# A two-layer decoder trunk: table stores by ScalarE, a later split of y, a shared start of two products, and a new order around the norms

## The chip, the cores and the metric

The kernel runs on one core of a Trainium2 chip. The core has five engines that work side by side, each in the order of its own queue: TensorE (PE in the profile; its weight loads are PEld), VectorE (DVE), ScalarE (ACT), GpSimd (POOL) and SyncE (SP), which only issues transfers here. Transfers (DMA) can be issued by SP, ACT and POOL. The metric is the device time of one execution in microseconds (us). TensorE's clock can be reduced by a throttle; the profile shows what was granted, as a share of full speed.

## The reference, cut to what matters

The input is x, 256 positions of 2048 float32 values. There are two layers; each ends in `x <- LayerNorm(alpha * x + mixer(x))`.

```python
# layer 0: one input projection, two groups of heads
z, xbc, dt, q, k, v, gate = split(x @ in0_w)
xs, b, c = split(silu(causal_conv4(xbc)))          # b, c: 512 columns each
y_a = rms_norm((ssd_scan(xs * dt, dt * a, b, c) + d * xs) * silu(z))
y_b = attention(rotary(q), rotary(k), v) * silu(gate)
x   = layer_norm(alpha * x + concat(y_a, y_b) @ out0_w)
# layer 1: diagonal complex state space
u, gate = split(x @ in1_w)
y   = gelu(s5_scan(u) + d * u)                     # 128 groups of 16 channels, 64 complex states
ga, gb = split(y @ glu_w)
x   = layer_norm(alpha * x + (ga * sigmoid(gb) * silu(gate)) @ out1_w)
```

## The kernel before, in words

**Weight units.** All weights are cut into 432 units of 256 rows by 512 columns (512 KB). Units 0 to 207 are the input projection of layer 0: 26 products of 8 units, in the order b, c, xs (four products), z (four) and then q, k, v, gate for four groups of heads. Units 208 to 271 are its output projection (4 products of 16), 272 to 335 the input projection of layer 1 (u, then the gate), 336 to 399 the GLU, 400 to 431 the last projection. `split_to(i)` prepares units up to i: SP loads `raw` (L222, four buffers), ScalarE copies it to `wh` (L225), the part that TensorE's rounded float32 type keeps, and VectorE subtracts to get the rest, `wl` (L227). Unit 0 is done in two halves (L217, L218), with x in two small pieces (`xpart`). x is split in the same way into a high part (tile A) and a rest (tile B). The pieces 1 to 7 of x (256 KB each) are loaded by `early` ahead of weight units 1 to 7.

**Products.** `product(kind, ...)` calls `split_to(unit + 3)` ahead of each unit, so preparation runs three units ahead of TensorE. For each tile three matmuls are made: high by high, high by rest, rest by high. Kind "w" (`wmm`, L288) has 24 matmuls of 256 columns for a unit, kind "x" (`xmm`, L271) has 12 of 512. A product's results lie in PSUM banks (`banks`), two alternating sets.

**Small work.** Everything else waits in two lists. `jobs` is emptied by `pump` between the units of the current product, `back` at a steady pace up to a goal. `run` pins the first instruction of a job behind the splits of the unit that is two ahead (`issue_after`). The order written down is not final: the framework's scheduler orders each engine's queue after a simulated timeline, within dependencies and pins.

**Layer-1 tables.** The state-space layer works in 16 blocks. During layer 0, `block_jobs(b)` builds each block's tables: `bars` (load of bc, then bb), `efs` (tables et and, in ob, F: L676 to L686), `pes` (transposes of et by TensorE, L694 and L698, ScalarE's copy into ob, L699, then VectorE's kt, L705) and, for odd b, `mts` (om). The tile ob has two buffers, et and om one. `phasor_job` computes the phasor tables on GpSimd (L624 to L640, tile c). The tables are stored to DRAM (wb) by transfers that GpSimd issues: ob at L706, om at L719, c at L640.

**Layer 1.** The steps of the state-space scan are in `back`, in order of a step number: for block b, `load` (wt) at 2b-2, `enc` at 2b (TensorE on the input um, L1128), `rec1` and `rec2` (VectorE's recurrence gt, L1140 to L1156), `dec` (L1169, L1173) and `act` at 2b+4. For every fourth block the finished outputs are loaded back by GpSimd at 2b+6 (`y_load`, L1198, tile ut) and split by ScalarE and VectorE at 2b+8 (`y_split`, L1206 and L1207).

**Norm 0.** The last product of layer 0 is `product_apart`: two halves t of positions, one after the other. When half t is done, `after0` adds the residual, takes statistics and scales x (`scaled`, L1010 and L1013, on tile D), `mid` transposes eight column blocks of t = 0 ahead of the last matmuls of t = 1 (`turned`, transposes at L358, ScalarE's copy at L1023 into tile C, VectorE's rest at L1027 into tile F). Then come `warm(WARM1)`, two transposes of t = 1, `warm(WARM2)`, and the first unit of layer 1, in which `rest0` stands between the matmuls of `wh` by high x and `wl` by high x and those of `wh` by low x. Further column blocks are scaled and transposed at units 1, 3 and 5 of that product (`later`). `warm(n)` makes n matmuls of zeros (64 x 64) whose result nobody reads (L367); `warm(WARM0)` also stands at the start.

**End.** `after1` does the last residual, statistics and the reciprocal, then `piece(3)`, which ScalarE and GpSimd compute (L1293 to L1295), and pieces 0 to 2, two passes each on VectorE (L1297, L1298); each is stored by SP or ACT (L1299).

Of the kernel before, what the change touches and what calls it, by code (L numbers as in the profile page):

```python
# [24 lines left out]
WARM0 = 70  # L25
WARM1 = 30
WARM2 = 4
# [66 lines left out]
def _layout(inp):  # L94
# [12 lines left out]
    cols = [b, c, xs, z]  # L107
    for h in range(4):
        cols += [m[:, 512 * h : 512 * h + 512] for m in (q, k, v, g)]
    a["wi0"] = np.concatenate([_chunk(m) for m in cols], 0)  # L110
# [49 lines left out]
def trunk(tc, io, out):  # L160
# [8 lines left out]
    with ExitStack() as top:  # L169
# [31 lines left out]
        early = {}  # L201
        splits = {}
        keep = [None, range(0)]

        def split_to(i):
            while nsplit[0] <= min(i, len(units) - 1):
                n = nsplit[0]
                if n in early:
                    early.pop(n)()
                raw = st.tile([P, UK, 512], F32, tag="raw", name=nm("raw"))  # L210
                if n == 0:
                    wh = st.tile([P, UK, 512], F32R, tag="wh", name=nm("wh"))
                    wl = st.tile([P, UK, 512], F32R, tag="wl", name=nm("wl"))
                    for k in range(UK):
                        xpart(k)
                        nc.sync.dma_start(raw[:, k, :], units[n][:, k * 512 : k * 512 + 512])
                        A.activation(wh[:, k, :], raw[:, k, :], AF.Copy)  # L217
# [4 lines left out]
                nc.sync.dma_start(raw.rearrange("p k n -> p (k n)"), units[n])  # L222
# [4 lines left out]
                splits[n] = (high, V.tensor_tensor(wl, raw, wh.bitcast(F32), op=OP.subtract))  # L227
# [45 lines left out]
        def wmm(ps, u, nu, hl, wpair, late=None):  # L273
            pv = [p.rearrange("p (f n) -> p f n", n=S) for p in ps]
            wh, wl = wpair
            steps = [(j, o) for j in range(UK) for o in range(4)]
            if u == nu - 1:
                steps = [(j, o) for o in range(4) for j in range(UK)]
            for terms in ((0, 2), (1,)) if late else ((0, 1, 2),):
                if late and terms == (1,):  # L280
                    late()
# [10 lines left out]
        def product(kind, hl, nu=CU, prelude=None, late=None):  # L292
            ps = banks()
            for u in range(nu):
# [4 lines left out]
                if kind == "w":  # L299
                    wmm(ps, u, nu, hl, wpair, late if u == 0 else None)  # L300
# [9 lines left out]
        def product_pair(hl, between, after):  # L310
            pss = [banks(), banks()]
            for lo, hi in ((0, CU - 2), (CU - 2, CU)):
# [11 lines left out]
                if lo == 0:  # L324
                    between()

# [35 lines left out]
        G.memset(idle.bitcast(F32), 0.0)  # L362

        def warm(n):
            px = aux()
            for i in range(n):
                T.matmul(px[:64, 0:64], idle, idle, start=i == 0, stop=i == n - 1)  # L367
# [13 lines left out]
        with ExitStack() as l0:  # L381
# [24 lines left out]
            for i in range(1, CU):  # L406
                early[i] = xpiece(i)
# [110 lines left out]
            ps = product("w", xhl)  # L518
            conv_jobs(ps, 0, bT)
            jobs.append(dt_mm)  # L520
            jobs.extend(dt_jobs())
            ps = product("w", xhl)
            conv_jobs(ps, 4, cT)
# [120 lines left out]
            def block_jobs(b):  # L644
# [25 lines left out]
                def efs():  # L670
# [3 lines left out]
                    ob = h["ob"] = pp.tile([P, 1024], F32, tag="ob", bufs=2, name=nm("ob"))  # L674
# [4 lines left out]
                    V.tensor_copy(et[:, :, :, 3], bb[:, 0])  # L679
                    cp = [bc[:, 3, 4 * i : 4 * i + 4, :].unsqueeze(3).to_broadcast([P, 4, 16, 4]) for i in range(2)]  # L680
# [7 lines left out]
                def pes():  # L688
# [17 lines left out]
                    nc.gpsimd.dma_start(wb[b][:, 0:1024], ob)  # L706

                def mts():
# [12 lines left out]
                return [bars, efs, pes, mts] if b % 2 else [bars, efs, pes]  # L721
# [270 lines left out]
        with ExitStack() as lt:  # L992
# [41 lines left out]
            def after0(ps, t):  # L1034
# [8 lines left out]
                jobs.append((lambda: scaled(1, 2, 2)) if t else (lambda: scaled(0, 4, 4)))  # L1043
# [20 lines left out]
            later = {1: [(1, 1)], 3: [(0, 2), (1, 2)], 5: [(0, 3), (1, 3)]}  # L1064
            first1 = product("w", x1hl, prelude=lambda u: [step(t, i) for t, i in later.get(u, [])], late=rest0)
# [3 lines left out]
        with ExitStack() as l1:  # L1069
# [139 lines left out]
            for b in range(16):  # L1209
# [55 lines left out]
        with ExitStack() as l2:  # L1265
# [16 lines left out]
            def after1(ps, t):  # L1282
                def first():
                    res1(ps, 3, t)
                    norm_stats(st1, mr1, t)()
                    V.scalar_tensor_tensor(mr1[:, t, 3:4], mr1[:, t, 0:1], -1.0, mr1[:, t, 2:3], op0=OP.mult, op1=OP.mult)

                def piece(i):
                    def go():
                        sl = slice(576 * i, min(576 * i + 576, D))  # L1290
                        xv = x1[:, t, sl]
                        if i == 3:
                            A.activation(xv, xv, AF.Identity, bias=mr1[:, t, 3:4], scale=mr1[:, t, 2:3])  # L1293
                            G.tensor_tensor(xv, xv, gb1[:, 0, sl], op=OP.mult)
                            G.tensor_tensor(xv, xv, gb1[:, 1, sl], op=OP.add)  # L1295
                        else:
                            V.scalar_tensor_tensor(xv, xv, mr1[:, t, 0:1], gb1[:, 0, sl], op0=OP.subtract, op1=OP.mult)  # L1297
                            V.scalar_tensor_tensor(xv, xv, mr1[:, t, 2:3], gb1[:, 1, sl], op0=OP.mult, op1=OP.add)  # L1298
                        (nc.sync if i % 2 else nc.scalar).dma_start(out[t * P : t * P + P, sl], xv)  # L1299
                    return go  # L1300

                jobs.append(first)
                jobs.extend([piece(i) for i in (3, 0, 1, 2)])
# [20 lines left out]
```

## Time and profile before

| | |
|---|---|
| median of 3 runs | 1374.88 us (1372.33 to 1376.38) |
| the profiled execution | 1374.04 us, of which the span is 1372.3 |
| mean granted TensorE clock | 0.992 |
| TensorE busy | 1351.2 us, 98% of the span |
| VectorE, ScalarE, GpSimd busy | 980.6, 673.5, 372.2 us |
| moved by DMA | 283 MB, mean 206 GB/s |

A row of the profile's groups has the line, the engine, the operation, the tile written and the tiles read (buffer numbers left out), the count, the busy time and the mean duration. A row of the timeline begins with the start and the duration in us and ends, where the engine was idle before it, with that idle time and what ended it. Matmuls are pipelined: their durations overlap, and the distance from start to start is what one costs.

### The profile page before, as it was taken

How to read it: one execution, taken by the hardware profiler on the slowest of the kernel's cores; microseconds unless marked ns; L12 is line 12 of the kernel's file. 1: busy time of each engine (PE TensorE's matmuls, PEld its weight loads, DVE VectorE, ACT ScalarE, POOL GpSimd, SP SyncE). 2: the span in 40 equal slices, each digit the busy share in tenths (PEclk: the TensorE clock that was granted, in tenths of full speed). 3: DMA queues.
4: the chain of work that ended last, by engine and by line, in shares of the span. 5: the costliest groups of instructions: out<-in, count | busy, mean ns of one | idle time of the engine just before them, and what ended most of it. 6: DMA issues, size and time to landing. Idle time of an engine off the chain costs nothing.

```text
span 1372.3 us, 25096 instructions
## 1 busy us (share of the span) xinstructions
PE 1351.2 (98%) x9918; PEld 1216.1 (89%) x9918; DVE 980.6 (71%) x1559; ACT 673.5 (49%) x869; POOL 372.2 (27%) x681
## 2 busy tenths in 40 slices
PE   9999999999999999999999899999999999999996
PEld 9999999998998998998988788899877788888885
DVE  5788746787688789779877766748878856555665
ACT  5565557754544544544554344344345545444441
POOL 0140000122016637737888200013333200000001
PEclk9999999999999999999999999999999999999998
DMA  8556655445546756755866678498889766666772
GB/s 304 179 156 197 182 169 155 160 146 171 174 150 209 240 175 214 234 182 190 278 193 194 221 226 305 143 304 264 278 225 303 219 207 186 197 184 187 256 216 77
DMA packets 79206, 283.02 MB, mean 206 GB/s; under 512 B 9840, under 2 KB 10480, under 8 KB 78576
## 3 DMA queue, kind: packets, MB, share of 16 engines
q1 hardware_dynamic: 68112, 239.33, 56.1%
q0 software_dynamic: 10400, 40.90, 8.8%
q8 instruction: 78, 1.28, 0.4%
q10 hardware_dynamic: 576, 1.18, 0.2%
q14 instruction: 40, 0.33, 0.1%
HBM read 260.41 MB, written 20.97 MB: 205 GB/s over the span
## 4 chain that ended last, share of the span: by engine, by line
PE 85%; POOL 7%; DVE 3%; DMA 2%; issue 2%; ACT 0%; POOLq 0%
PE main L288 42%; PE main L271 35%; POOL c L635 3%; POOL c L637 1%; POOL c L638 1%; DMA wb<-c 1%; PE aux L358 1%; DVE wl L227 1%; PE aux L791 1%; PE enc L1128 1%; PE dec L1173 1%; PE aux L367 1%; DMA ut<-yd 1%; PE aux L761 0%; PE aux L698 0%
## 5 line engine op out<-in xcount | busy, mean ns | idle before, releaser
L227 DVE TENSOR_TENSOR wl<-raw,wh 128x1024 fp32r<-128x1024 f32 x431 | 537.3, 1248 | 334.7 <-ACT wh L225 328.7
L225 ACT ACTIVATE wh<-raw 128x1024 fp32r<-128x1024 f32 x431 | 455.8, 1059 | 581.0 <-PE main L271 270.7
L288 PE MATMUL main<-A,wh 128*128 128x256 f32 x1408 | 402.5, 286 | 0.0
L288 PE MATMUL main<-A,wl 128*128 128x256 f32 x1408 | 400.1, 284 | 0.0
L288 PE MATMUL main<-B,wh 128*128 128x256 f32 x1408 | 399.8, 284 | 0.0
L288 PEld LDWEIGHTS main<-A,wh 128*128 128x128 f32 x1408 | 270.5, 192 | 0.6 <-issue 0.2
L288 PEld LDWEIGHTS main<-B,wh 128*128 128x128 f32 x1408 | 270.5, 192 | 0.4
L288 PEld LDWEIGHTS main<-A,wl 128*128 128x128 f32 x1408 | 270.5, 192 | 0.3 <-issue 0.2
L271 PE MATMUL main<-wh,A 128*128 128x512 f32 x512 | 201.5, 394 | 0.0
L271 PE MATMUL main<-wh,B 128*128 128x512 f32 x512 | 201.1, 393 | 0.0
L271 PE MATMUL main<-wl,A 128*128 128x512 f32 x512 | 200.9, 392 | 0.0
L271 PE MATMUL main<-wh,C 128*128 128x512 f32 x384 | 152.4, 398 | 0.0
L271 PE MATMUL main<-wh,F 128*128 128x512 f32 x384 | 150.5, 392 | 0.0
L271 PE MATMUL main<-wl,C 128*128 128x512 f32 x384 | 150.3, 391 | 0.0
L271 PEld LDWEIGHTS main<-wh,B 128*128 128x128 f32 x512 | 96.7, 189 | 20.2
L271 PEld LDWEIGHTS main<-wl,A 128*128 128x128 f32 x512 | 96.8, 189 | 20.0 <-issue 0.2
L271 PEld LDWEIGHTS main<-wh,A 128*128 128x128 f32 x512 | 96.7, 189 | 19.9 <-issue 0.2
L635 POOL TENSOR_TENSOR c<-c 128x8 f32<-128x8 f32 (+2 forms) x192 | 99.3, 535 | 19.2 <-DMA wb<-c 11.8
L271 PEld LDWEIGHTS main<-wh,C 128*128 128x128 f32 x384 | 72.5, 189 | 15.7
L271 PEld LDWEIGHTS main<-wh,F 128*128 128x128 f32 x384 | 72.4, 188 | 15.3
L271 PEld LDWEIGHTS main<-wl,C 128*128 128x128 f32 x384 | 72.5, 189 | 14.5
L801 POOL TENSOR_TENSOR ssq<-ssq,c 128x256 f32<-128x256 f32 x16 | 17.6, 1100 | 210.2 <-ACT c L799 209.6
(281 smaller groups left out, 1690.0 us busy)
## 6 DMA issues: line engine op xcount, KB each, us to landing
raw<-in_wi SPq DMA_DIRECT2D x271, 512.0 KB, 4.1
raw<-in_wo SPq DMA_DIRECT2D x96, 512.0 KB, 4.3
raw<-in_wglu SPq DMA_DIRECT2D x64, 512.0 KB, 3.7
wt<-wb POOLq DMA_DIRECT2D x16, 896.0 KB, 8.1
wb<-ob POOLq DMA_DIRECT2D x16, 512.0 KB, 6.0
bc<-in_s5bc SPq DMA_DIRECT2D x16, 256.0 KB, 4.2
wb<-c POOLq DMA_DIRECT2D x16, 256.0 KB, 3.6
wb<-om POOLq DMA_DIRECT2D x16, 128.0 KB, 3.4
```

The source lines that it names most:

```text
L225: high = A.activation(wh, raw, AF.Copy)
L227: splits[n] = (high, V.tensor_tensor(wl, raw, wh.bitcast(F32), op=OP.subtract))
L271: T.matmul(ps[o], l[:, k, sl], r[:, j, :], start=start and i == 0, stop=stop and i == 2)
L288: T.matmul(pv[o // 2][:, o % 2, :], l[:, j, sl], r[:, k, :], start=first and i == 0 and o % 2 == 0, stop=end and i == 2 and o % 2 == 1, sk ...
L358: end = T.transpose(dst[:, i * P : i * P + P], s, ident)
L367: T.matmul(px[:64, 0:64], idle, idle, start=i == 0, stop=i == n - 1)
L635: G.tensor_tensor(p[:, :, :, 0:m], cs[:, :, :, 1 : m + 1], cs[:, i, :, n : n + 1].unsqueeze(1).to_broadcast([P, 2, 4, m]), op=OP.mult)
L637: G.tensor_tensor(cs[:, 0, :, n + 1 : n + 1 + m], p0[:, 0, :, 0:m], p1[:, 1, :, 0:m], op=OP.subtract)
L638: G.tensor_tensor(cs[:, 1, :, n + 1 : n + 1 + m], p0[:, 1, :, 0:m], p1[:, 0, :, 0:m], op=OP.add)
L791: T.matmul(yo, xs[:, 0, xc], df[:, i, 0:256], start=True, stop=False)
L801: G.tensor_tensor(ssq, ssq, jk[:, f, :], op=OP.add)
L1128: T.matmul(px[64 * at : 64 * at + 64, i, r * 128 + q * 64 : r * 128 + q * 64 + 64], wt[64 * i : 64 * i + 64, a * P + 64 * r : a * P + 64 * ...
```

## The change

1. The numbers of zero matmuls go from 70, 30 and 4 to 8, 14 and 3, and each now has 128 rows by 512 columns, from a broadcast of the same zero tile. VectorE rather than GpSimd clears that tile.
2. The products b and c become `product_two`: their first four units alternate (b0, c0, b1, c1, ...), then the rest of b, then the rest of c. Their weights lie in DRAM in that order. The pieces of x are loaded ahead of units 2, 4, 6, 8, 9, 10 and 11, each behind the previous raw load. In the first four units the matmuls on `wl` stand behind all those on `wh`; in unit 0 this is done for each of its two row blocks. The results of b are worked on after unit 11, those of c after unit 15.
3. `run` pins a job behind the raw load of the unit two ahead as well.
4. `efs` is cut in two, `efs` (et) and `fcs` (F), and ob is taken in `fcs`. The stores of ob and om are issued by ScalarE.
5. Around norm 0, the column blocks 8 to 11 of t = 0 are scaled behind blocks 4 to 7 of t = 0, ahead of the residual of t = 1; they were scaled ahead of unit 3 of the next product. Their transposes stay there. `rest0` keeps its place.
6. `y_split` goes from step 2b+8 to 2b+9.
7. At the end, the pieces have new edges (0, 566, 1132, 1696, 2048). VectorE takes piece 0's first pass, the reciprocal and the bias at once, then the rest in a fixed order; ScalarE and GpSimd take piece 3, now 352 columns; its store is SP's last.

```diff
-WARM0 = 70
-WARM1 = 30
-WARM2 = 4
+WARM0 = 8
+WARM1 = 14
+WARM2 = 3
+PAIRED = 4
+EDGE = (0, 566, 1132, 1696, 2048)
...
+    first = np.stack([b[:PAIRED], c[:PAIRED]], 1).reshape(-1, P, UK * 512)
+    a["wi0"] = np.concatenate([first, b[PAIRED:], c[PAIRED:]] + [_chunk(m) for m in cols], 0)
...
-                    early.pop(n)()
+                    with tc.issue_after(loaded[-1].ins):
+                        early.pop(n)()
...
-                splits[n] = (high, V.tensor_tensor(wl, raw, wh.bitcast(F32), op=OP.subtract))
+                splits[n] = (loaded[-1], high, V.tensor_tensor(wl, raw, wh.bitcast(F32), op=OP.subtract))
...
+        def product_two(hl, after):
+            pss = [banks(), banks()]
+            order = [(n, u) for u in range(PAIRED) for n in range(2)] + [(n, u) for n in range(2) for u in range(PAIRED, CU)]
+            for at, (n, u) in enumerate(order):
+                split_to(at + 3)
+                parts = (((0, 1), (0, 1)), ((0, 1), (2,)))
+                if at == 0:
+                    parts = tuple(((j,), t) for j in range(UK) for t in ((0, 1), (2,)))
+                wmm(pss[n], u, CU, hl, ready.pop(at), parts if at < 4 else WHOLE)
+                unit[0] += 1
+                pump(CU - 1 - u)
+                if u == CU - 1:
+                    after(pss[n], n)
...
-                T.matmul(px[:64, 0:64], idle, idle, start=i == 0, stop=i == n - 1)
+                T.matmul(px, idle[:, 0:1].to_broadcast([P, P]), idle.unsqueeze(1).to_broadcast([P, 8, 64]), start=i == 0, stop=i == n - 1)
...
-                early[i] = xpiece(i)
+                early[2 * i if i < PAIRED else PAIRED + i] = xpiece(i)
...
-                    ob = h["ob"] = pp.tile([P, 1024], F32, tag="ob", bufs=2, name=nm("ob"))
...
+                def fcs():
+                    bc = h["bc"]
+                    ob = h["ob"] = pp.tile([P, 1024], F32, tag="ob", bufs=2, name=nm("ob"))
...
-                    nc.gpsimd.dma_start(wb[b][:, 0:1024], ob)
+                    nc.scalar.dma_start(wb[b][:, 0:1024], ob)
...
-                        nc.gpsimd.dma_start(wb[b - 1 + i][:, 1024:1280], om[:, 256 * i : 256 * i + 256])
+                        nc.scalar.dma_start(wb[b - 1 + i][:, 1024:1280], om[:, 256 * i : 256 * i + 256])
...
-                jobs.append((lambda: scaled(1, 2, 2)) if t else (lambda: scaled(0, 4, 4)))
+                jobs.extend([lambda: scaled(1, 2, 2)] if t else [lambda: scaled(0, 4, 4), lambda: scaled(0, 8, 4)])
...
-            later = {1: [(1, 1)], 3: [(0, 2), (1, 2)], 5: [(0, 3), (1, 3)]}
-            first1 = product("w", x1hl, prelude=lambda u: [step(t, i) for t, i in later.get(u, [])], late=rest0)
+            later = {1: [(1, 1)], 3: [(1, 2)], 5: [(0, 3), (1, 3)]}
+            first1 = product("w", x1hl, prelude=lambda u: [turned(0, 8, 4) if u == 3 else None] + [step(t, i) for t, i in later.get(u, [])], first=(((0, 1), (0, 2)), rest0, ((0, 1), (1,))))
...
-                    at(2 * b + 8, lambda b=b: y_split(b // 4))
+                    at(2 * b + 9, lambda b=b: y_split(b // 4))
...
+                    done = norm_stats(st1, mr1, t)
+                    op = V.scalar_tensor_tensor(piece(0), piece(0), mr1[:, t, 0:1], gb1[:, 0, span(0)], op0=OP.subtract, op1=OP.mult)
+                    with tc.issue_after(op.ins):
+                        done()
+                        op = V.scalar_tensor_tensor(mr1[:, t, 3:4], mr1[:, t, 0:1], -1.0, mr1[:, t, 2:3], op0=OP.mult, op1=OP.mult)
...
+                    nc.sync.dma_start(out[t * P : t * P + P, span(3)], piece(3))
```

More of the change, by code (lines that the diff above doesn't have):

```diff
@@ L201, in trunk @@
         early = {}
+        loaded = []
         splits = {}
@@ L290, in wmm, with product @@
                                  skip_group_check=True)
-        def product(kind, hl, nu=CU, prelude=None, late=None):
+        def product(kind, hl, nu=CU, prelude=None, first=WHOLE):
             ps = banks()
@@ new lines, in first @@
+                    G.tensor_tensor(xv, xv, gb1[:, 1, span(3)], op=OP.add)
+                    for i in range(3):
+                        xv = piece(i)
+                        with tc.issue_after(op.ins):
+                            if i:
+                                V.scalar_tensor_tensor(xv, xv, mr1[:, t, 0:1], gb1[:, 0, span(i)], op0=OP.subtract, op1=OP.mult)
+                            op = V.scalar_tensor_tensor(xv, xv, mr1[:, t, 2:3], gb1[:, 1, span(i)], op0=OP.mult, op1=OP.add)
+                        (nc.sync if i % 2 else nc.scalar).dma_start(out[t * P : t * P + P, span(i)], xv)
```

64 lines of the change are left out of this document (29 added, 35 removed).

## The prediction

> **What bounds the kernel now.** I read the page first, then the waits of TensorE, then the granted clock in windows around each wait, and last the timeline at six places. The page, busy time by engine:
>
> ```profile
> PE 1351.2 (98%) x9918; PEld 1216.1 (89%) x9918; DVE 980.6 (71%) x1559; ACT 673.5 (49%) x869; POOL 372.2 (27%) x681
> ```
>
> TensorE is the bound: an edit pays only where it takes away TensorE's idle time, its work, or its time at half clock. The largest of its waits (line, releaser: total, times, longest; two more stand below at their places):
>
> ```profile
> PE aux L694 <- DVE et L678: 4.1, 1, 4.1
> ```
>
> Each of the three has a tail at half clock. Windows (stretch, length, then busy time and count of PE, PEld, DVE, ACT, POOL, then the granted clock, the DMA share and GB/s):
>
> ```profile
> 755.00:759.20 4.20, 0.07 (x2) 0.06 (x2) 2.48 (x4) 0.00 (x0) 3.95 (x10) 1.00 0.10 41
> 759.20:762.60 3.40, 3.40 (x24) 2.74 (x25) 3.40 (x4) 0.60 (x1) 2.86 (x4) 0.50 0.54 123
> 762.60:766.00 3.40, 3.40 (x10) 2.63 (x9) 3.11 (x7) 1.06 (x1) 0.53 (x1) 0.50 0.91 340
> 875.30:878.70 3.40, 3.40 (x18) 3.40 (x18) 3.24 (x6) 0.06 (x1) 0.00 (x0) 0.50 0.00 0
> 1005.00:1008.40 3.40, 3.40 (x32) 2.70 (x24) 3.37 (x6) 0.00 (x0) 0.56 (x1) 0.50 0.76 223
> ```
>
> In 755.00 to 759.20 TensorE did next to nothing, and the two stretches of 3.4 us behind it ran at clock 0.50. Half the clock for 3.4 us costs at most 3.4 / 2 = 1.7 us of work: 3.4 behind 755, 1.7 behind norm 0, 1.7 behind 1001.
>
> **The change, part by part.**
>
> *Start.* Eight zero matmuls of 512 columns stand for seventy tiny ones, and the products of b and c take the pieces of x in turns.
>
> ```profile
> 0.94 7.68 PE L367 MATMUL aux<-idle 128*64 128x64 f32 x70 [0.94 <-POOL idle L362]
> 4.06 0.63 ACT L217 ACTIVATE wh<-raw 128x512 fp32r<-128x512 f32 x1 [0.60 <-DMA raw<-in_wi]
> 8.79 0.41 PE L288 MATMUL main<-B,wh 128*128 128x256 f32 x1
> 9.00 0.41 PE L288 MATMUL main<-A,wl 128*128 128x256 f32 x1
> 9.84 1.06 ACT L225 ACTIVATE wh<-raw 128x1024 fp32r<-128x1024 f32 x1 [2.50 <-DMA raw<-in_wi]
> 11.80 1.06 ACT L225 ACTIVATE wh<-raw 128x1024 fp32r<-128x1024 f32 x1 [0.39 <-DMA raw<-in_wi]
> ...
> 21.45 0.28 PE L288 MATMUL main<-A,wh 128*128 128x256 f32 x1
> 21.57 0.28 PE L288 MATMUL main<-B,wh 128*128 128x256 f32 x1
> ```
>
> The tiny matmuls hold the first product until 0.94 + 7.68 = 8.62 (its second matmul starts at 8.79), though its first weights are split at 4.06 + 0.63 = 4.69. Its matmuls start 0.21 apart at first (8.79, 9.00), later 0.12 (21.45, 21.57). After, the first product can start at about 4.7. The weights of unit 1 landed at 9.84 as the sixth transfer (1536 KB so far) and the next two transfers (768 KB) by 11.80, 1.96 later. As the fifth (1280 KB) they land one 256 KB piece earlier: 0.65 us at that pace, up to three times that if the first transfers ran slower. I take 8.3 and add the split, 1.06: unit 1 starts at 9.4, and three more units of 24 x 0.12 = 2.88 follow it without a wait, so that unit 4 starts at 9.4 + 3 x 2.88 = 18.05 instead of 21.45: gain 3.4. Bounds: 2.2 (landing at 9.5) and 4.0 (landing at 7.7). If the zeros leave the clock low, a half-clock stretch can fall on units 1 to 3: 3.4 - 1.7 = 1.7.
>
> The taps of b and c now stand within eight units and no longer in sixteen.
>
> ```profile
> L509 DVE SCALAR_TENSOR_TENSOR a<-main,params,a 128x255 f32<-128x255 f32 (+2 forms) x12 | 5.3, 475 | 0.1
> L227 DVE TENSOR_TENSOR wl<-raw,wh 128x1024 fp32r<-128x1024 f32 x10 | 12.2, 1224 | 5.5 <-ACT wh L225 5.4
> ```
>
> Twelve taps (5.3) and four splits (4 x 1.22 = 4.9) make 10.2 of the 11.5 us of VectorE in four units, and the next product needs those banks behind them. Cost 0 to 1.5 (one unit's half), taken 0.5 since it just fits.
>
> *Table stores by ScalarE.*
>
> ```profile
> 739.99 0.42 DVE L686 TENSOR_TENSOR ob<-ob,tm 128x256 f32<-128x256 f32 x1
> 742.83 1.06 ACT L225 ACTIVATE wh<-raw 128x1024 fp32r<-128x1024 f32 x1 [1.68 <-PE main L271]
> 750.66 0.55 POOL L706 DMA_DIRECT2D wb<-ob  x1
> 756.72 1.58 DVE L684 TENSOR_TENSOR ob<-bc,lap 128x256 f32<-128x256 f32 x2 [5.11 <-DMA wb<-ob]
> 759.17 1.05 PE L694 MATMUL aux<-consts,et 128*128 128x128 f32 x4 [4.13 <-DVE et L678]
> 761.13 0.80 PE L271 MATMUL main<-wh,A 128*128 128x512 f32 x1
> 766.49 0.39 PE L271 MATMUL main<-wl,A 128*128 128x512 f32 x1
> 766.71 0.39 PE L271 MATMUL main<-wh,B 128*128 128x512 f32 x1
> ...
> wb<-ob POOLq DMA_DIRECT2D x16, 512.0 KB, 6.0
> ```
>
> The tile ob is finished at 739.99 + 0.42 = 740.41, but GpSimd's queue, in the next block's phasors, issues its store at 750.66. Landing takes 6.0; VectorE waits 5.11 us to write an ob again, et is queued behind that, and TensorE stands 4.1 us. Then come twenty small matmuls and thirteen main ones at half clock; the thirteen take 766.49 - 761.13 = 5.4 instead of 13 x 0.22 = 2.9, which is 2.5, and I add 0.4 for the small ones: 2.9 (at most 3.4). After, ScalarE issues the store behind its own last copy to ob, some 9 us earlier, and it has landed before VectorE comes. Besides, ob is taken in a step of its own behind et, so that a late store would hold the next table and not TensorE's et. Gain 4.1 + 2.9 = 7.0.
>
> Added to ScalarE: 32 issues (16 of ob, 16 of om), by the nearest row 0.55 each, 17.6 in all. Queued behind each is the split of a weight unit. ScalarE is 49% busy and idles 1.68 before the split at 742.83, waiting for the buffer that TensorE still reads. An issue of 0.55, or a pair of 1.1, lies in that. I take 0; with the cover gone 17.6. GpSimd's queue loses the same 32 issues, so phasors and the wt loads behind them come no later.
>
> The Trainium skill ("DMA: Bandwidth & Descriptors", section "Issuing engines are not separate DMA queues") speaks against this part: every issuer feeds the same 16 DMA engines, and another issuer saves only its sequencer's time, usually small beside the transfer. By it the part would give about nothing, and the sum 7.0 less. This case's rows differ in where the time goes: 10.2 us pass between the finished tile and the issue, 6.0 in the transfer.
>
> *Norm 0.*
>
> ```profile
> 870.37 1.88 PE L367 MATMUL aux<-idle 128*64 128x64 f32 x30
> 873.52 0.44 PE L358 MATMUL aux<-consts,D 128*128 128x128 f32 x2 [1.27 <-DVE D L1013]
> 882.44 1.04 PE L358 MATMUL aux<-consts,D 128*128 128x128 f32 x8
> 883.23 0.49 PE L288 MATMUL main<-C,wh 128*128 128x256 f32 x2
> 866.12 0.75 DVE L1010 SCALAR_TENSOR_TENSOR D<-D,mr,row 128x512 f32<-128x512 f32 x1
> 869.38 1.29 DVE L1027 TENSOR_TENSOR F<-aux,C 128x512 fp32r<-128x512 f32 x2 [1.73 <-ACT C L1023]
> ```
>
> Behind 870.37 the last half of the norm runs on VectorE, and the transposes wait for it until 873.52. Fourteen zeros of 512 columns (14 x 0.227 = 3.2) end at 873.55: neither gain nor loss by themselves. They can win the half-clock stretch behind it, at most 1.7. The scaling moved ahead of t = 1 is two passes of 0.75, and VectorE idles 1.73 before 869.38; without that cover it costs 1.5. Four transposes (883.23 - 882.44 = 0.79 for eight, so 0.4) change their place only. Gain 1.2, less than 1.7 because the remaining 0.4 us gap and the longer last zeros may eat some; bounds -0.4 (zeros too long, clock not held) and 2.0.
>
> *The split of y one step later.*
>
> ```profile
> 998.89 1.06 ACT L1206 ACTIVATE A<-ut 128x1024 fp32r<-128x1024 f32 x1 [6.76 <-DMA ut<-yd]
> 1004.32 0.68 PE L1173 MATMUL dec<-gt,wt 64*64 64x63 f32 x16 [2.92 <-DVE gt L1155]
> ```
>
> ScalarE stands 6.76 us before this split until its load lands at 998.89, VectorE with it, and the recurrence that writes gt is queued behind. One step later is two units, about 5.5 us, and then the load has landed when the split's turn comes. Gone: 2.9 of idle and, of 1.7 behind it, 1.6: 4.5. Bounds 0 (the wait stays, by another split) and 4.6. Late next: y's halves, needed only by the next stage's products.
>
> *Encoder.* By the new order the first enc stands a unit earlier: 920.50 - 2.88 = 917.6.
>
> ```profile
> 912.14 0.72 POOL L1094 DMA_DIRECT2D um<-ud  x1 [4.98 <-DMA ud<-ut]
> ...
> 920.50 0.32 PE L1128 MATMUL enc<-um,wt 64*64 64x64 f32 x2
> ...
> um<-ud POOLq DMA_DIRECT2D x16, 128.0 KB, 6.2
> ```
>
> Its load lands at 912.14 + 6.2 = 918.3 or a little later, since a second one is issued behind it. Cost 1.0; bounds 0 and 2.7 (1.0 and a half-clock stretch).
>
> *End.*
>
> ```profile
> 1362.96 2.26 DVE L1297 SCALAR_TENSOR_TENSOR D<-D,mr,A 128x576 f32<-128x576 f32 x3
> 1365.41 2.87 DVE L1298 SCALAR_TENSOR_TENSOR D<-D,mr,A 128x576 f32<-128x576 f32 x3
> 1367.74 1.25 POOL L1295 TENSOR_TENSOR D<-D,A 128x320 f32<-128x320 f32 x1
> ```
>
> GpSimd's piece ends last, at 1368.99. After, it starts behind one first pass and no longer three (1.5 earlier) and has 352 columns for 320 (2.7 x 0.1 = 0.3 longer): 1367.8. But VectorE's six passes over 1696 columns, 0.98 x (2.26 + 2.87) = 5.0 plus the two small steps, end at 1368.3 to 1369. Gain 0.2; bounds -0.4 and 1.0.
>
> Sum: 3.4 - 0.5 + 7.0 + 1.2 + 4.5 - 1.0 + 0.2 = 14.8. The profiled execution took 1374.04 (span 1372.3), 0.8 below the median of 1374.88; 1374.04 - 14.8 = 1359.2.
>
> **Rivals.** *The zeros don't hold the clock.* The start gives 1.7 and norm 0 -0.4: 1359.2 + 1.7 + 1.6 = 1362.5. For it: the seventy tiny ones ran for 7.7 us, and the matmuls behind them still stood 0.21 apart. Against: they had an eighth of the columns. The Trainium skill ("TensorE: Matmul & The Clock Gate", Part 1, "The HAM clock gate") lets the clock rise after a window of busy array and fall after an idle one, some 3.4 us long. The stretches of 3.4 us here agree with that length; by it 3.2 us of zeros at norm 0 leave too little idle for a fall.
>
> *A stall stays or moves.* The table stores change nothing because the wait for ob returns in another block, 1359.2 + 7.0 = 1366.2; or y's split still meets its load, 1359.2 + 4.5 = 1363.7. For it: only one block in sixteen and one split in four show such a wait, so it hangs on the order of that moment. Against: both get several us more room than they lacked.
>
> *Slower: ScalarE becomes late.* The ob store waits on ScalarE's queue for VectorE's half of ob, with a weight split behind it. Whatever the hold exceeds the slack of 1.68 by, TensorE waits, in each of 16 blocks. The point at which it decides is 14.8 / 16 = 0.93 us over, a hold of 2.6; at 1.2 over, 1359.2 + 16 x 1.2 = 1378.4, and half-clock tails come on top. For it: ScalarE works in order, as 6.76 us at 998.89 shows. Against: that wait of 6.76 cost TensorE nothing on its weights, as no wait on wh or wl is among its largest; at 740 VectorE's half (740.41) was done before ScalarE's next split ended.
>
> **Chances.** The forecast 0.56, its own range 1356 to 1361.5. Zeros don't hold the clock 0.14. A stall stays or moves 0.20 (stores 0.12, y 0.08). Slower 0.06. Several at once, ending within 0.3% (1370.8 to 1379.0, about what a measurement of this kernel can tell from no change) 0.04. The low end has every part at its better bound: 1359.2 - 0.6 - 0.5 - 0.5 - 0.8 - 0.1 - 1.0 - 0.8 = 1354.9, rounded to 1354.5; the high end is the table stall kept and half of the clock's loss, 1368. Faster 0.90, same 0.04, slower 0.06.
>
> **What would show it.** Right: unit 4 starts near 18 us; no store is issued 10 us behind its tile; clock 1.00 from 750 to 770, 872 to 882 and 1000 to 1010; ScalarE's split of y has no idle for its load. Wrong: a TensorE wait on wh or wl behind a store on ScalarE, a new stretch at clock 0.50 (I would look first at the first enc and at the third product), or VectorE waiting for ob in another block.

## The result and the profile after

The changed kernel takes 1371.55 us (median, 1369.62 to 1372.53), the kernel before, beside it, 1374.34 (1372.33 to 1376.41). The ratio is 0.9977, interval 0.9969 to 0.9986: 0.2% faster, some 3 us. The forecast was 1359.2, in a range of 1354.5 to 1368. The profiled execution of the changed kernel took 1371.28 (span 1369.5).

The page of the changed kernel, busy time by engine, and below it the waits of TensorE (line, releaser: total, times, longest). Lines of the changed kernel are numbered anew: L288 became L298, L271 became L277, L227 became L233, L509 (a tap) became L533, L1027 became L1056.

```profile
PE 1345.3 (98%) x9839; PEld 1207.5 (88%) x9839; DVE 984.7 (72%) x1560; ACT 671.9 (49%) x869; POOL 363.5 (27%) x648
```
```profile
PE main L298 <- DVE a L533: 7.4, 2, 7.1
PE main L298 <- DVE F L1056: 1.3, 1, 1.3
PE main L298 <- ACT wh L231: 1.0, 2, 0.7
PE aux L391 <- DVE idle L386: 1.0, 1, 1.0
PE main L277 <- DVE wl L233: 0.6, 2, 0.3
```

Both waits that stood at the head of this list before, for et and for gt, are gone. In their place stands one of 7.1 us that was not there: a main product waits for VectorE's taps.

**Where the time went, stretch by stretch.** ScalarE's split of a unit waits for a buffer that TensorE frees, so the start of the same unit's split in both traces shows how far one TensorE is ahead of the other. For unit 24, for example, it stands at 74.20 before and at 71.04 after: 3.16 ahead. Differences of these, after minus before, are taken where neighbouring units agree, since single splits stray; each row is the change within its stretch:

| stretch | forecast | measured |
|---|---|---|
| start (to unit 24) | -3.4 | -3.2 |
| taps of b and c and what is queued with them (units 24 to 126) | +0.5 | +10.0 |
| small waits (units 126 to 228) | 0 | +1.1 |
| table store (units 228 to 245) | -7.0 | -7.4 |
| norm 0 (units 255 to 287) | -1.2 | +0.6 |
| first enc (units 287 to 300) | +1.0 | +0.4 |
| split of y (units 306 to 322) | -4.5 | -4.9 |
| last units and the end | -0.2 | +0.6 |
| sum | -14.8 | -2.8 (spans: -2.8) |

The new stall, in the timeline (start, duration) of the changed kernel: TensorE alone, then the taps (L533), ScalarE's part of them (L530) and the works that precede them.

```profile
106.92 0.28 PE L298 MATMUL main<-A,wl 128*128 128x256 f32 x1
114.34 0.55 PE L298 MATMUL main<-A,wh 128*128 128x256 f32 x1 [7.14 <-DVE a L533]
```
```profile
84.19 1.28 ACT L580 ACT_TABLE_LOAD   x1 [1.08 <-DMA a<-in_s5p]
85.93 0.42 DVE L581 TENSOR_TENSOR a<-a,a 128x256 f32<-128x256 f32 x1 [3.92 <-ACT a L580]
90.32 1.47 POOL L494 TENSOR_TENSOR ew<-ew 32x256 f32<-32x256 f32 x1
92.78 0.41 DVE L500 SCALAR_TENSOR_TENSOR ew<-ew,dw 32x256 f32<-32x256 f32 x1
95.34 0.42 ACT L506 ACTIVATE cumhl<-dw 32x256 fp32r<-32x256 f32 x1 [2.67 <-DVE dw L505]
100.04 1.02 ACT L530 ACTIVATE a<-main,params 128x256 f32<-128x256 f32 x2
100.73 0.48 DVE L533 SCALAR_TENSOR_TENSOR a<-main,params,a 128x255 f32<-128x255 f32 x1
113.33 0.86 DVE L533 SCALAR_TENSOR_TENSOR a<-main,params,a 128x254 f32<-128x254 f32 x2
114.65 0.47 DVE L533 SCALAR_TENSOR_TENSOR a<-main,params,a 128x253 f32<-128x253 f32 x1
```

The fifth product (the third of xs, from unit 32) takes the banks that the third product left some 27 us earlier, when it was done. Those banks come free with the third product's twelve taps. The taps run from 100.73 to 115.12, because on ScalarE's and VectorE's queues they stand behind the chain of dt (GpSimd's polynomial to 91.8, then L500 to L506) and the trigonometry of the tables (L580 and on). TensorE could have gone on at 107.04. The same taps before, and the two engines' waits ahead of them:

```profile
78.62 1.28 ACT L554 ACT_TABLE_LOAD   x1
85.14 0.41 DVE L476 SCALAR_TENSOR_TENSOR ew<-ew,dw 32x256 f32<-32x256 f32 x1 [1.01 <-POOL ew L470]
91.83 0.57 ACT L506 ACTIVATE a<-main,params 128x256 f32<-128x256 f32 x1
109.99 0.47 DVE L509 SCALAR_TENSOR_TENSOR a<-main,params,a 128x253 f32<-128x253 f32 x1
```

There the fifth product began at 109.25 (its first matmul, found by counting), and the last tap ended at 110.46.

```profile
109.25 0.28 PE L288 MATMUL main<-A,wh 128*128 128x256 f32 x1
```

TensorE went on without a wait, so its matmuls into the second bank came behind 110.46; the trace doesn't name the bank of a matmul, so how much room there was can't be read. The change brought TensorE to this place 2.2 us earlier (107.04 for 109.25) and the last tap 4.7 us later (115.12 for 110.46). The clock falls during the stall and is at half behind it; windows (stretch, length, busy time of PE, PEld, DVE, ACT, POOL, clock, DMA share, GB/s):

```profile
107.00:114.30 7.30, 0.20 (x2) 0.00 (x0) 7.30 (x16) 1.51 (x2) 0.00 (x0) 0.80 0.68 211
114.30:117.70 3.40, 3.36 (x16) 3.39 (x17) 2.67 (x11) 2.49 (x3) 0.00 (x0) 0.50 0.54 161
```

VectorE is busy for all of the 7.3 us. The 7.3, half of the 3.4 us at clock 0.50 (1.7) and two waits of 0.5 and 0.2 ahead of it (for L500 and for a tap) make 9.7 of the +10.0 of the table.

### The profile page after: what moved, and what is told of

Read it like the earlier page. It is cut to its first block, busy times and chain, and to the rows that moved or that the text cites. A ratio compares the mean times of both kernels' runs of the same rounds, so it can differ in the third digit from the quotient of the medians.

```text
span 1369.5 us, 24907 instructions
## 1 busy us (share of the span) xinstructions
PE 1345.3 (98%) x9839; PEld 1207.5 (88%) x9839; DVE 984.7 (72%) x1560; ACT 671.9 (49%) x869; POOL 363.5 (27%) x648
## 4 chain that ended last, share of the span: by engine, by line
PE 90%; DVE 6%; DMA 1%; issue 1%; ACT 1%; SPq 0%; DVEq 0%; ACTq 0%
PE main L277 43%; PE main L298 40%; DVE wl L233 2%; PE aux L382 1%; PE enc L1157 1%; PE aux L820 1%; PE dec L1202 1%; PE aux L727 1%; DMA raw<-in_wi 1%; DMA bc<-in_s5bc 1%; PE aux L932 1%; PE aux L900 1%; PE dec L1198 0%; PE aux L790 0%; DVE a L533 0%
## 5 line engine op out<-in xcount | busy, mean ns | idle before, releaser
L233 DVE TENSOR_TENSOR wl<-raw,wh 128x1024 fp32r<-128x1024 f32 x431 | 537.2, 1249 | 326.4 <-ACT wh L231 324.1
L298 PE MATMUL main<-A,wh 128*128 128x256 f32 x1408 | 401.9, 286 | 8.4 <-DVE a L533 7.4
L298 PE MATMUL main<-B,wh 128*128 128x256 f32 x1408 | 399.0, 284 | 0.0
L298 PE MATMUL main<-A,wl 128*128 128x256 f32 x1408 | 395.0, 284 | 0.0
L298 PEld LDWEIGHTS main<-A,wh 128*128 128x128 f32 x1408 | 270.8, 192 | 10.4 <-issue 7.9
L298 PEld LDWEIGHTS main<-B,wh 128*128 128x128 f32 x1408 | 270.9, 192 | 0.4
L298 PEld LDWEIGHTS main<-A,wl 128*128 128x128 f32 x1408 | 268.6, 192 | 0.2 <-issue 0.2
L277 PE MATMUL main<-wl,A 128*128 128x512 f32 x512 | 200.4, 391 | 0.6 <-DVE wl L233 0.6
L277 PE MATMUL main<-wh,A 128*128 128x512 f32 x512 | 200.4, 392 | 0.0
L277 PE MATMUL main<-wh,B 128*128 128x512 f32 x512 | 200.0, 391 | 0.0
L277 PE MATMUL main<-wh,C 128*128 128x512 f32 x384 | 152.0, 397 | 0.0
L277 PE MATMUL main<-wh,F 128*128 128x512 f32 x384 | 150.0, 391 | 0.0
L277 PE MATMUL main<-wl,C 128*128 128x512 f32 x384 | 149.8, 390 | 0.0
L277 PEld LDWEIGHTS main<-wl,A 128*128 128x128 f32 x512 | 96.2, 188 | 21.0 <-DVE wl L233 1.4
L277 PEld LDWEIGHTS main<-wh,B 128*128 128x128 f32 x512 | 96.1, 188 | 19.9
L277 PEld LDWEIGHTS main<-wh,A 128*128 128x128 f32 x512 | 96.2, 188 | 19.8 <-issue 0.2
L661 POOL TENSOR_TENSOR c<-c 128x8 f32<-128x8 f32 (+2 forms) x192 | 105.3, 567 | 25.5 <-DMA wb<-c 18.0
L277 PEld LDWEIGHTS main<-wh,C 128*128 128x128 f32 x384 | 72.1, 188 | 15.6
L277 PEld LDWEIGHTS main<-wh,F 128*128 128x128 f32 x384 | 72.1, 188 | 15.4
L277 PEld LDWEIGHTS main<-wl,C 128*128 128x128 f32 x384 | 72.1, 188 | 14.2
```

The lines of the kernel that those rows point to most:

```text
L233: splits[n] = (loaded[-1], high, V.tensor_tensor(wl, raw, wh.bitcast(F32), op=OP.subtract))
L277: T.matmul(ps[o], l[:, k, sl], r[:, j, :], start=start and i == 0, stop=stop and i == 2)
L298: T.matmul(pv[o // 2][:, o % 2, :], l[:, j, sl], r[:, k, :], start=first and i == 0 and o % 2 == 0, stop=end and i == 2 and o % 2 == 1, sk ...
L661: G.tensor_tensor(p[:, :, :, 0:m], cs[:, :, :, 1 : m + 1], cs[:, i, :, n : n + 1].unsqueeze(1).to_broadcast([P, 2, 4, m]), op=OP.mult)
```

## The experiments

Three theories stood. A: the order of the queues makes the stall; dt's chain and the trigonometry start four units later than before, and the taps are behind them. B: the load of s5p alone, 5.5 us later, makes it. C: VectorE has too much work before that point, whatever its order. Medians are compared with the kernel before, run beside them.

**The load of s5p earlier.**

```diff
+            jobs.appendleft(lambda: nc.sync.dma_start(s5p, io["s5p"]))
             def trig_job():
-                nc.sync.dma_start(s5p, io["s5p"])
```

> The changed kernel, but the load of s5p is issued on SP some seven units ahead of the job that uses it, so that ScalarE (1.08 us idle before L580) and VectorE (3.92 us idle before L581) need not stand for it. Theory A (order of the queues: the taps of the first xs product stand behind the dt chain and the trig work, both four units later than before, and the bank of the third xs product waits for them): VectorE then stands for GpSimd's end of the dt chain at about 91.8 instead, so the 7.1 us wait of TensorE at L298 falls by at most 1 us; about 1371. Theory B (the late load alone makes the stall): the wait falls by 3.9 to about 3.2 us, about 1367.5. Theory C (VectorE simply has too much work before that point): no change, 1371.5.

1371.05, ratio 0.9970 (0.9959 to 0.9980): as the changed kernel. The wait stays (first row, waits of TensorE), and so does most of VectorE's idle time ahead of the trigonometry (second row, timeline), 2.87 of 3.92 us: ScalarE itself comes late to that job.

```profile
PE main L298 <- DVE a L533: 7.1, 2, 6.9
```
```profile
84.69 0.66 DVE L582 TENSOR_TENSOR a<-a,a 128x256 f32<-128x256 f32 x1 [2.87 <-ACT a L581]
```

B falls.

**The tables later.**

```diff
-            jobs.extend([trig_job, table_job])
...
             for j in range(4):
                 ps = product("w", xhl)
                 xs_jobs(ps, j)
+                if j == 0:
+                    jobs.extend([trig_job, table_job])
```

> The changed kernel, but the trig and table jobs are queued behind the first xs product's taps and no longer ahead of them. Theory A: the taps end before their bank is wanted again, the 7.1 us wait and its half-clock tail (2.5 to 3) go, about 1361.8. Theory B: the wait for s5p then holds nothing that TensorE needs, about 1361.8 too. Theory C: VectorE's work is only moved, and the wait comes back at the fourth xs product or the first z product with most of its size: 1368 to 1371.

1362.59, ratio 0.9913 (0.9892 to 0.9934). The 7.1 us wait is gone, and no other took its place in the products of layer 0; C falls. Here the first enc waits 2.1 us for its data instead.

**One product after the other.** The weights of b and c in their old order, x in one piece for each unit, the rest of the change kept.

```diff
...
-                early[2 * i if i < PAIRED else PAIRED + i] = xpiece(i)
+                early[i] = xpiece(i)
...
-            product_two(xhl, bc_jobs)
+            bc_jobs(product("w", xhl), 0)
+            bc_jobs(product("w", xhl), 1)
```

> The changed kernel with the products b and c one after the other and x in one piece for each unit, as before; all other parts of the change stay. Theories A and B: the dt chain and the trig work start four units earlier, no wait of TensorE at 107, the gain of the start (3.2) is lost in part: 1363 to 1365. Theory C: the wait stays, shortened only by what TensorE comes later: about 1371.

1364.87, ratio 0.9933 (0.9911 to 0.9957). No wait at the fifth product. The gain of the start is lost too (unit 24 is 0.4 us behind the kernel before): TensorE waits 2.1 us for unit 1, and the clock falls behind it (window).

```profile
12.00:15.40 3.40, 3.30 (x17) 3.30 (x18) 3.13 (x5) 2.85 (x4) 0.00 (x0) 0.57 1.03 409
```

**dt later.**

```diff
                 if n == 0:
-                    jobs.append(dt_mm)
-                    jobs.extend(dt_jobs())
...
                 xs_jobs(ps, j)
+                if j == 0:
+                    jobs.append(dt_mm)
+                    jobs.extend(dt_jobs())
```

> The changed kernel, but the dt product and its chain are queued behind the first xs product's taps, eight units or more later than in the changed kernel. Theory A: with the dt chain gone from ahead of the taps only the trig work and its load are left there, the wait falls to 0 to 4 us: 1362 to 1367. Theory B: the wait stays at 7: 1371. Theory C: less VectorE work ahead (about 5 us), wait about 2 to 3: 1366.

1361.20, ratio 0.9905 (0.9884 to 0.9926). No wait at the fifth product: the taps now run from 81.14 (first row below) to 97, while the trigonometry still precedes them in the list of jobs. So taking either dt's chain or the trigonometry from ahead of the taps is enough. Between 102 and 117 VectorE is as busy as in the changed kernel, and TensorE doesn't stop (window).

```profile
81.14 0.48 DVE L533 SCALAR_TENSOR_TENSOR a<-main,params,a 128x255 f32<-128x255 f32 x1
```
```profile
107.00:112.00 5.00, 5.00 (x44) 4.96 (x43) 4.82 (x19) 2.71 (x4) 0.00 (x0) 1.00 0.45 138
```

**Only the two products in turns**, on the kernel before, with its tiny zero matmuls.

```diff
...
+            product_two(xhl, bc_jobs)
-            ps = product("w", xhl)
-            conv_jobs(ps, 0, bT)
...
-            ps = product("w", xhl)
-            conv_jobs(ps, 4, cT)
```

> The kernel before with only the two first products taking x in turns (and dt, c and b work queued as there); zero matmuls, stores, pins and all else as before. If the late queueing of dt and trig makes the stall: VectorE ends the taps at about 114.6 whatever TensorE does; TensorE, not earlier at the start (the 70 tiny matmuls end at 8.6), reaches their bank at about 110.4 and waits 4 us, with a half-clock tail 6 to 7 in all: about 1381. If the stall needed the stores on ScalarE or the new pin: 1374 to 1375.

1388.66, ratio 1.0101 (1.0081 to 1.0120): slower by more than expected. The part alone makes the stall, so neither the stores, the pin of jobs nor the earlier start is needed for it (TensorE is 0.1 us behind the kernel before at unit 24). My figure for its size was wrong: TensorE comes there 3.2 us later than in the changed kernel and still waits 7.15.

```profile
117.50 0.55 PE L297 MATMUL main<-A,wh 128*128 128x256 f32 x1 [7.15 <-DVE a L532]
```

The taps thus have no fixed time; the small work is handed out between units, so its end shifts with TensorE. The kernel with only the zero matmuls (below) shows the same: its TensorE reaches the fifth product 2.2 us before the kernel before, its last tap ends 2.2 us earlier too (108.29), and there is no wait. The stall is worth +9.8 by the units; another +3.6 comes between units 255 and 287, at norm 0 (waits of 0.9 for F and 0.7 for C), of which the next run tells more.

**Only the stores by ScalarE**, on the kernel before, with `efs` cut in two and ob taken behind et as in the change.

```diff
...
-                    nc.gpsimd.dma_start(wb[b][:, 0:1024], ob)
+                    nc.scalar.dma_start(wb[b][:, 0:1024], ob)
...
-                        nc.gpsimd.dma_start(wb[b - 1 + i][:, 1024:1280], om[:, 256 * i : 256 * i + 256])
+                        nc.scalar.dma_start(wb[b - 1 + i][:, 1024:1280], om[:, 256 * i : 256 * i + 256])
```

> The kernel before with one part of the change: efs cut in two, ob taken behind et, the stores of ob and om issued by ScalarE. If the stall at 755 came from the late issue on GpSimd's queue, its 4.1 us and its half-clock tail go (7.9 us by the unit times of the changed kernel), and the small new waits between units 126 and 204 (1.5 us there) come: 1374.9 - 7.9 + 1.5 = 1368.5. If another block makes the same wait, or the small waits grow in place of it: 1373 to 1375.

1372.34, ratio 0.9970 (0.9959 to 0.9980), where about 1368.5 was expected; the profiled span equals that of before (1372.2 and 1372.3). This profiled execution, 1374.02, is the second slowest of its ten; by the medians some 4 us of the gain are left. The stall at 755 is gone: unit 228 is 0.5 us behind the kernel before, unit 255 is 7.0 ahead. Then, in this execution, it is given back: 3.6 between units 255 and 287, and 3.4 at the split of y. At norm 0 (first row below) rest0's two transposes come at 870.11, 3.4 us behind the zero matmuls that start at 866.75; before, they came 0.8 behind them (874.53 after 873.72). Neither zeros nor order were changed in the program there, so the scheduler placed them anew. TensorE then waits 0.9 for F and 0.8 for C. At the split of y ScalarE now waits 9.69 us for the same load, where it was 6.76, and TensorE stops twice.

```profile
866.75 0.45 PE L367 MATMUL aux<-idle 128*64 128x64 f32 x4
870.11 0.63 PE L358 MATMUL aux<-consts,D 128*128 128x128 f32 x2
...
991.89 0.76 POOL L1201 DMA_DIRECT2D ut<-yd  x1 [9.71 <-issue]
998.44 1.06 ACT L1209 ACTIVATE A<-ut 128x1024 fp32r<-128x1024 f32 x1 [9.69 <-DMA ut<-yd]
999.83 0.34 PE L1172 MATMUL dec<-um,wt 64*64 64x64 f32 x8 [2.08 <-ACT ys L1182]
1003.88 0.82 PE L1176 MATMUL dec<-gt,wt 64*64 64x63 f32 x16 [3.71 <-DVE gt L1158]
```

The load lands at 998.44, within half a microsecond of 998.89 before, though TensorE arrived 3.4 us sooner.

**Only the split of y later**, on the kernel before.

```diff
-                    at(2 * b + 8, lambda b=b: y_split(b // 4))
+                    at(2 * b + 9, lambda b=b: y_split(b // 4))
```

> The kernel before with the split of y one step later and nothing else. If the 2.9 us wait at the dec line and the half-clock stretch behind it come from the split's place alone: 4.5 to 4.9 us less, about 1370.2. If it needs the other parts too (the load issued earlier): 1374 to 1375.

1368.63, ratio 0.9942 (0.9926 to 0.9958). By the spans of the profiled executions 1367.1 against 1372.3, 5.1 less; by the medians some 8, but the kernel before took 1376.96 beside it, more than beside the changed kernel. The wait for gt is gone and the clock stays up.

```profile
1000.00:1004.00 4.00, 4.00 (x63) 3.13 (x62) 4.00 (x7) 1.43 (x2) 1.49 (x4) 1.00 0.99 363
```

**Only the zero matmuls**, on the kernel before.

```diff
-WARM0 = 70
-WARM1 = 30
-WARM2 = 4
+WARM0 = 8
+WARM1 = 14
+WARM2 = 3
-                T.matmul(px[:64, 0:64], idle, idle, start=i == 0, stop=i == n - 1)
+                T.matmul(px, idle[:, 0:1].to_broadcast([P, P]), idle.unsqueeze(1).to_broadcast([P, 8, 64]), start=i == 0, stop=i == n - 1)
```

> The kernel before with only the zero matmuls changed: 8, 14 and 3 of 512 columns for 70, 30 and 4 of 64, the tile cleared by VectorE. If they hold the clock: 1.00 instead of 0.50 at 875 to 878 (1.7 us won), but rest0's transposes come 16 matmuls later and the third unit of layer 1 waits 1.3 for F (1.5 lost); at the start at most 0.4, since x still comes in one piece for each unit: 1374 to 1375, the clock row is what tells. If zeros are no work to the throttle: clock 0.50 at 875 to 878 as before, 1375 to 1376.

1375.13, ratio 1.0000 (0.9988 to 1.0012). TensorE is 3.9 us ahead of the kernel before at norm 0. The zeros hold the clock over the norm's gap: it is 1.00 at 871.4 to 874.8, the work that stood at 0.50 before (875.3 to 878.7). But then TensorE waits 0.7 for D and 1.3 for F, and the clock falls at about 880.7:

```profile
871.40:874.80 3.40, 3.40 (x31) 3.40 (x31) 1.39 (x3) 1.22 (x2) 0.00 (x0) 1.00 0.02 5
874.80:878.20 3.40, 2.74 (x24) 2.53 (x23) 3.40 (x5) 1.70 (x3) 0.00 (x0) 1.00 0.11 16
878.20:881.60 3.40, 2.06 (x14) 1.78 (x13) 3.40 (x6) 0.67 (x2) 0.00 (x0) 0.87 0.62 207
881.60:885.00 3.40, 3.40 (x22) 3.40 (x21) 2.51 (x4) 0.48 (x1) 0.23 (x1) 0.62 0.21 86
```

At the start they win 2.2 by the units, more than the 0.4 I allowed, and around norm 0 they lose 2.5 (units 255 to 287). In one_by_one the same zeros won nothing at the start; the difference is the wait for unit 1, 2.1 us there, behind which the clock fell again, and 1.1 here, behind which it stayed at 1.00.

**The old order around norm 0**, on dt later.

```diff
-                jobs.extend([lambda: scaled(1, 2, 2)] if t else [lambda: scaled(0, 4, 4), lambda: scaled(0, 8, 4)])
+                jobs.append((lambda: scaled(1, 2, 2)) if t else (lambda: scaled(0, 4, 4)))
```

> The kernel with dt later (1361.2), with the scaling and the transposes around norm 0 in the order of before, but the new zero matmuls kept. If the new order makes the 1.3 us wait for F at the third unit of layer 1, that wait goes and the clock stays at 1.00: about 1359.7. If the zeros make it (they put TensorE's transposes later): 1361.

1362.52, ratio 0.9899 (0.9881 to 0.9918), not told apart from dt later. The 1.3 us wait for F stays. So the order of the scaling does not make it; zeros_only, with the old order, has the same wait.

**The old end**, on dt later.

> The kernel with dt later (1361.2), with the end of before (pieces of 576, reciprocal behind three first passes). If the new end costs 0.6 to 0.7 (unit times are 3.4 less than before's at the end, the span only 2.8): 1360.5. If that is the spread of a single execution, 1361.2; if the new end is better, 1361.5 to 1362.

1360.92, ratio 0.9887 (0.9869 to 0.9904). By the medians this can't be told from dt later; by the traces the loss at the end is gone (from unit 420 to the end of the span 0.0, against +0.6 in dt later).

**Both mended**: the old end, and the first matmuls of layer 1 pinned behind the transposes of rest0, once on dt later, once on tables later.

```diff
-first=(((0, 1), (0, 2)), rest0, ((0, 1), (1,)))
+first=(rest0, ((0, 1), (0, 2)), ((0, 1), (1,)))
...
                 if callable(part):
-                    part()
+                    held = part()
...
+                        with ExitStack() as pin:
+                            if held is not None:
+                                pin.enter_context(tc.issue_after(held.ins))
```

> The kernel with dt later (1361.2), with the end of before (0.7 less) and with the first matmuls of layer 1 pinned behind rest0's transposes (1.5 less): 1359.0. If the wait for F was set by VectorE's work and not by the transposes' place, it comes back at the next unit: 1360.5.

> The kernel with the tables later (1362.6), with the end of before (0.7 less) and with the first matmuls of layer 1 pinned behind rest0's transposes (the wait for F, 1.3 and its gap, 1.5 less): 1360.4 if the wait of 2.1 at the first enc and its tail stay, 1356.5 if they go.

1359.34, ratio 0.9888 (0.9873 to 0.9903), and 1359.57, ratio 0.9891 (0.9876 to 0.9906). In both the wait for F is gone, the clock is 1.00 through the norm, and TensorE's longest wait is 1.1 and 1.5 at the first enc (for a load; the second row's releaser is the input um). They beat the kernel before and the changed one, by some 16 and 12 us.

```profile
PE enc L1162 <- DMA raw<-in_wi: 1.1, 1, 1.1
```
```profile
PE enc L1163 <- DMA um<-ud: 1.5, 1, 1.5
```

## Why the prediction was wrong, and where it was right

**The step that failed** is the second half of *Start*: "The taps of b and c now stand within eight units and no longer in sixteen ... Cost 0 to 1.5 ..., taken 0.5 since it just fits". It measured +10.0. The step counted VectorE's instructions of two products against four units. It left out what is queued with them: dt's product and its chain, handed out after unit 11 and no longer after unit 7, the trigonometry, and the taps of the third product, which are behind both in the order of two engines. And it followed only the taps of b and c; the fourth product, which needs the banks of c, waited for them 0.2 us (at 79.94), while the fifth waited 7.1 for the taps of the third. The rows that should have been looked at are those of the kernel before at the fifth product: it began at 109.25, the last tap of the third ended at 110.46, so there was no room for several us of work queued anew ahead of these taps. The earlier start is not the cause: two_only has the wait without it, and zeros_only has 2.2 of its 3.2 us without the wait.

**Start**: right in mechanism; that unit 4 begins at 18.29 (forecast 18.05) is partly luck: unit 1 began at 8.99, 0.4 us sooner than forecast, and units 1 to 3 took 9.3 where 8.64 was forecast (TensorE waits 0.3 us for the weights of unit 2, at 12.43). The first product begins at 4.68 (4.7).

```profile
0.99 3.78 PE L391 MATMUL aux<-idle 128*128 128x512 f32 x8 [0.99 <-DVE idle L386]
4.68 0.58 PE L298 MATMUL main<-A,wh 128*128 128x256 f32 x1
5.48 0.35 PE L298 MATMUL main<-B,wh 128*128 128x256 f32 x1
5.67 0.27 PE L298 MATMUL main<-A,wh 128*128 128x256 f32 x1
5.79 0.28 PE L298 MATMUL main<-B,wh 128*128 128x256 f32 x1
```

The matmuls are 0.12 apart from 5.67 on. So the rival that zeros don't hold the clock falls.

**Table stores**: 7.4 for 7.0. The store is issued 0.1 us behind its tile (744.59 + 0.41, then 745.07), and VectorE waits for ob no more.

```profile
744.59 0.41 DVE L715 TENSOR_TENSOR ob<-ob,tm 128x256 f32<-128x256 f32 x1
745.07 0.33 ACTq L735 DMA_DIRECT2D wb<-ob  x1
760.26 0.74 DVE L713 TENSOR_TENSOR ob<-bc,lap 128x256 f32<-128x256 f32 x2
```

Two edits do this together, and they were not tried apart: the next ob is now written behind et, at 760.26, and the old store had landed by 756.72. So the new order of `efs` might have removed TensorE's wait without the move to ScalarE.

The rule of the Trainium skill ("DMA: Bandwidth & Descriptors", section "Issuing engines are not separate DMA queues"), by which the part would give about nothing, doesn't decide here. It prices an issue; the time was in the queue ahead of it. The issues on ScalarE were hidden, as I took them: no TensorE wait of over 0.7 on wh came. Between units 126 and 228, though, +1.1 came in small pieces that I had at 0 (waits of 0.2 and 0.3 for wl among them). The kernels with the stores on ScalarE have +0.4 to +1.25 there, y_only, zeros_only and two_only less than 0.1; so it goes with the stores, the cut of efs or the pin, and stores_only (+0.4) has no pin. What in that part makes it wasn't tried.

**Split of y**: right, 4.9 for 4.5, and by itself 5.1. ScalarE still waits 1.83 us for the load (at 1002.86), against the sign that I had named, but TensorE doesn't. What I missed is that the part is bound to the stores: without it, 3.4 of their 7.4 are lost here (stores_only).

**Norm 0**: the mechanism was half right. The clock is held, but the step said the transposes "change their place only". Rest0's two transposes now come behind 16 main matmuls (876.94, before at 874.53), as they do in zeros_only, with the old order, and in stores_only, with the old order and the old zeros: the scheduler puts them there. VectorE's passes for the next column blocks follow their result, and TensorE waits 1.34 for F at 884.55.

```profile
874.80:878.20 3.40, 3.40 (x29) 3.28 (x28) 0.92 (x4) 0.46 (x2) 0.00 (x0) 1.00 0.02 5
```
```profile
876.94 0.38 PE L382 MATMUL aux<-consts,D 128*128 128x128 f32 x2
884.55 0.39 PE L298 MATMUL main<-F,wh 128*128 128x256 f32 x1 [1.34 <-DVE F L1056]
```

With the transposes pinned ahead, that wait is gone, and the stretch gives -1.4 instead of +0.6 (unit 255 to 287: -10.43 to -11.82), near the forecast of -1.2.

**Encoder**: +0.4 for 1.0, within its bounds.

**End**: -0.2 forecast, +0.6 measured, outside the bounds (to +0.4). VectorE ends last, as I wrote. The last passes of the changed kernel in the timeline:

```profile
1361.37 1.43 POOL L1321 TENSOR_TENSOR D<-D,A 128x352 f32<-128x352 f32 x1 [8.02 <-ACT D L1320]
1362.05 1.35 DVE L1328 SCALAR_TENSOR_TENSOR D<-D,mr,A 128x566 f32<-128x566 f32 x1
1362.88 1.31 POOL L1322 TENSOR_TENSOR D<-D,A 128x352 f32<-128x352 f32 x1
1363.32 1.46 DVE L1327 SCALAR_TENSOR_TENSOR D<-D,mr,A 128x564 f32<-128x564 f32 x1
1364.82 0.81 DVE L1328 SCALAR_TENSOR_TENSOR D<-D,mr,A 128x564 f32<-128x564 f32 x1
```

Two passes beside GpSimd take 1.35 and 1.46, the third alone 0.81. The Trainium skill ("GPSIMD Engine Reference", section "1. Specifications") has GpSimd's SBUF interfaces shared with VectorE and names contention with VectorE instructions of two SBUF inputs; these passes have two, and the rows agree. Before, the three second passes took 2.87 where the three first ones took 2.26: one of them met GpSimd. Starting earlier, GpSimd meets two. And the store that ends last is now one of 282 KB (2.7 us to landing), where it was one of 160 KB (2.1). My step had neither; how the loss divides between them wasn't tried.

**The rivals.** That a stall stays or moves had 0.20, with a time of 1363.7 to 1366.2. It moved, but not as told: not in the tables or at y, where both stalls went, but to a place I had named only as the one to look at ("the third product"; it was the fifth). The slower rival, ScalarE late for the weights, didn't come.

## What to carry to other kernels

Where small work is handed out between units, the first question on a move is not whether an engine has room for it, but what is queued behind it and who needs that, two products on: read the last release of each bank or buffer against its next use, and ask what the move puts ahead of that release in the queues of the engines that make it. A stage that ends with another engine's load or chain takes back what is won ahead of it, so edits at two stalls in a row must be priced together. A warm clock is worth only what the next gap leaves of it.

## What the runs showed of the hardware that I had not expected

Large zero matmuls raised the clock, small ones did not. Seventy of 64 columns, issued without a gap for 7.68 us, left the following matmuls 0.21 us apart for 3 us more; eight of 512 columns, 3.78 us, were followed by matmuls at 0.12 from 5.67 us on, 4.7 us behind the first zero, and in zeros_only from 7.00 on, 6.0 us behind it. The large ones also load twice as many columns of weights; which of the two sizes counts wasn't tried. The Trainium skill ("TensorE: Matmul & The Clock Gate", Part 1, "The HAM clock gate") says that a window of activity of about 3.4 us raises the clock, whatever the number of matmuls. For the large ones the traces agree in the main (the rise comes 4.7 and 6.0 us behind the first), for the tiny ones the trace doesn't: 7.68 us of them were not enough.
